# Modulation chunks 2 to 5 of a hybrid diffusion block: from scaled row sums and TensorE column sums to VectorE dots of transposed rows

## Chip, cores, metric

The kernel runs on one core of one Trainium2 chip. The metric is the device time of one execution in microseconds (us). All matrices are float32; each product is made of three float32r matmuls (high part by high part, high by low, low by high).

## What is computed

One layer of a diffusion transformer on 512 tokens of width 1024, with 256 context tokens. The part that matters here is the modulation: a conditioning row `c` of 1024 numbers goes through a SiLU and a 1024 by 6144 matrix, and the result is cut into six chunks of 1024 that shift, scale and gate the two halves of the layer.

```python
silu_c = jax.nn.silu(c)
mx = jnp.split((silu_c @ w_mod[l] + b_mod[l])[:, None, :], 6, axis=-1)
hx = modulate(rms_norm(x, g_mix[l]), mx[0], mx[1])
...
x = x + mx[2] * merge_branches(y_conv_x, att_x, gt_x, w_out[l])
hx2 = modulate(rms_norm(x, g_ffn[l]), mx[3], mx[4])
x = x + mx[5] * swiglu(hx2, w_13[l], w_2[l])
return rms_norm(x, g_final)
```

Chunks 0 and 1 are needed at the start, 2 at the output projection of the merge, 3 and 4 before the feed-forward part, 5 only at its second matrix.

## The kernel before

The layer is computed transposed: a tile holds 128 channels on the partitions and 512 tokens along the free axis. A weight tile is 128 by 1024 float32 (512 KB). `wtile` (L130) loads it on SP's DMA queue into one of three raw buffers `wr`, ScalarE casts it in two halves to float32r (`wh`, L118), and VectorE subtracts to get the low halves (`wl`, L122). There are six `wh` and six `wl` halves, so three tiles of weights. `gemm` (L138) then runs 8 times 3 matmuls of 128x512 (`mm3`, L134 to L136), 24 to a tile.

The order of the program around the change is:

1. eight attention heads, with the convolution's work between them; the last head leaves `o_t[7]` (L523);
2. the gate part: the remaining gates, each a tile of 24 matmuls and a Tanh (`gate`, L540 to L547); the sum of the eight convolution tiles (L857), its mean by a ones matmul (L860), then subtraction, squares and sums (L863 to L867), the variance's column sums (L187), `rstd_cols` (L170, and a power on GpSimd L172), and the broadcast of the result by another ones matmul (L177, L182);
3. the merge: the convolution tiles are scaled (L887) and pass a SiLU (L889), the heads are split in high and low parts (L101, L102); eight tiles with `w_o` (L896 to L901), eight with `w_pw` (L903 to L915), eight with `w_out` (L918 to L978);
4. the feed-forward part: 22 pairs of tiles with `w_13` (L1064 to L1076), then eight tiles of 22 products with `w_2`, and the final norm.

The code of 2, of 3 up to the fifth `w_out` tile, and of 4 up to the last `w_2` tile is not ordered by hand: the tile framework's scheduler puts each engine's instructions in an order of its own at compile time, by what it reckons to be ready, and gives out buffers in that order. Each engine then works its list in that order, and so does SP with its DMAs.

Modulation chunks 2 to 5 are `w_mod25[0]` to `[3]`. `mod_steps` (L202) makes a chunk in 16 steps: for each of 8 rows of input channels and each of two halves of 512 output channels, VectorE writes one column of a buffer of tag `p` (a copy from `after`, L207, which holds the step back until `after` exists), SP loads 256 KB (L208), and VectorE multiplies by a per-partition scalar of `sc` and adds to one of two accumulators (L210; L212 for the first). `mod_cols` (L220) then sums each accumulator over the partitions: 8 matmuls of 128x1 with a column of ones (L223; the profile shows two passes of each), and VectorE adds the bias (L225). The steps are handed out by `pump`: `MODS` says how many after each gate, each `w_o` tile and each `w_pw` tile (3, 3, 3), and `MCOLS` after which `w_pw` tile each chunk is finished. Chunk 5 is made by `mod_chunk` after the fifth pair of the feed-forward part (L1073) and finished after the fifteenth (L1075).

`row_dot` (L264) exists already: at the start chunk 1 is made by it. It multiplies a 128x1024 tile of transposed weights by a row that every partition holds, and sums along the row in the same instruction (`accum_out`). `md_tile` (L234) gives its buffers: tag `ur`, four of them, which are also used by the convolution's tap rows and by three of the residual tiles `x2` (L934).

Of the kernel before, what the change touches and what calls it, by code (L numbers as in the profile page):

```python
# [10 lines left out]
F32 = mybir.dt.float32  # L11
F32R = mybir.dt.float32r
AF = mybir.ActivationFunctionType
ALU = mybir.AluOpType
# [4 lines left out]
P = 128  # L19
D = 1024  # L20
KD = D // P
# [9 lines left out]
NB0 = 2  # L31
NB1 = 7
W_BUFS = 6
MODS = (3, 3, 3)
MCOLS = (2, 4, 7)
UPAD = 544
UW = 520
# [18 lines left out]
def block_kernel(ctx: ExitStack, tc: tile.TileContext, I, out):  # L56
    nc = tc.nc
    pe, act, dve, pool, sp = nc.tensor, nc.scalar, nc.vector, nc.gpsimd, nc.sync
# [24 lines left out]
    def slot(dt=F32, n=512):  # L83
        return ap.tile([P, n], dt, tag="act", name=nm("a"))
# [68 lines left out]
    def v(name, i=None, n=1):  # L153
        a, b = VEC[name]
        return vec[:, a:b] if i is None else vec[:, a + i:a + i + n]

    ones = cp.tile([P, P], F32, name="ones")
# [3 lines left out]
    sc = cp.tile([P, 16], F32, name="sc")  # L161
    act.activation(sc, vec[:, 0:16], AF.Silu)
    bm1 = cp.tile([P, 16], F32, name="bm1")
    dve.tensor_scalar(out=bm1[:, 0:8], in0=v("b_mod", 8, 8), scalar1=1.0, scalar2=None, op0=ALU.add)
    dve.tensor_scalar(out=bm1[:, 8:16], in0=v("b_mod", 32, 8), scalar1=1.0, scalar2=None, op0=ALU.add)
    modc = cp.tile([P, 32], F32, name="modc")
# [23 lines left out]
    def ps_x(n=512):  # L190
        return pp.tile([P, 512], F32, tag="x", name=nm("px"), bufs=4)[:, 0:n]
# [7 lines left out]
    def wide():  # L199
        return bp.tile([P, 768], F32, tag="p", name=nm("p"))  # L200

    def mod_steps(c, after, acc):  # L202
        acc += [slot(), slot()]
        for kc in range(8):
            for e in range(2):
                md = wide()[:, 0:512]
                dve.tensor_copy(out=md[:, 0:1], in_=after[:, 0:1])  # L207
                sp.dma_start(out=md, in_=I["w_mod25"][c, kc, :, e * 512:e * 512 + 512])  # L208
                if kc:
                    dve.scalar_tensor_tensor(out=acc[e], in0=md, scalar=sc[:, 2 * kc:2 * kc + 1], in1=acc[e], op0=ALU.mult, op1=ALU.add)  # L210
                else:
                    dve.tensor_scalar(out=acc[e], in0=md, scalar1=sc[:, 2 * kc:2 * kc + 1], scalar2=None, op0=ALU.mult)  # L212
                yield

    def mod_chunk(c, after):
        acc = []
        pump(mod_steps(c, after, acc), 99)
        return acc

    def mod_cols(c, acc):  # L220
        ps = ps_x(8)
        for i in range(8):
            pe.matmul(ps[:, i:i + 1], lhsT=acc[i // 4][:, (i % 4) * P:(i % 4 + 1) * P], rhs=ones[:, 0:1], start=True, stop=True)  # L223
        col = modc[:, c * 8:c * 8 + 8]
        dve.tensor_tensor(out=col, in0=ps, in1=bm1[:, 8:16] if c == 2 else v("b_mod", 16 + c * 8, 8), op=ALU.add)  # L225
        if c == 0:
            dve.tensor_scalar(out=col, in0=col, scalar1=0.5, scalar2=None, op0=ALU.mult)
        elif c == 2:
            dve.tensor_tensor(out=col, in0=col, in1=v("g_ffn", 0, 8), op=ALU.mult)
# [7 lines left out]
    def pads(tag):  # L237
        return bp.tile([P, 2, UPAD], F32R, tag=tag, name=nm(tag), bufs=1)

    def row_tile(j):  # L240
        t = pads(("u", "y")[j]).bitcast(F32).rearrange("p a b -> p (a b)")[:, 0:D]
        sp.dma_start(out=t, in_=I["crow"][:, j * D:j * D + D])
        return t

# [45 lines left out]
    def pump(it, n):  # L290
        for _ in range(n):
            if next(it, it) is it:
                break
# [4 lines left out]
    conv, o_t = [None] * KD, [None] * H  # L298
# [256 lines left out]
    with tc.manual_schedule(engines={ET.PE, ET.DVE, ET.Activation, ET.Pool, ET.SP}):  # L555
        for k in range(KD):
            t = slot()
# [24 lines left out]
        for k in range(KD):  # L582
# [17 lines left out]
            t = temp()  # L600
# [175 lines left out]
        for k in range(KD + 1):  # L776
            if k < KD:
                t = temp(C)
# [5 lines left out]
            if k:  # L784
                dve.scalar_tensor_tensor(out=hcs[k - 1][1], in0=ts[k - 1], scalar=ssc[:, k - 1:k], in1=hcs[k - 1][0].bitcast(F32),
                                         op0=ALU.add, op1=ALU.subtract)
# [63 lines left out]


    if True:
        maccs = [[], [], []]
        mods_it = itertools.chain(*(mod_steps(i, o_t[7], maccs[i]) for i in range(3)))
        tot = slot()
        for i in range(1, KD):
            dve.tensor_tensor(out=tot, in0=conv[0] if i == 1 else tot, in1=conv[i], op=ALU.add)  # L857
# [45 lines left out]
        for i in range(KD):  # L903
            w = wtile(I["w_pw"][i])
            ps = ps_x()
            gemm(ps, w, yc)
            t = sg_conv[i]
            dve.scalar_tensor_tensor(out=t, in0=t, scalar=1.0, in1=ps, op0=ALU.add, op1=ALU.mult)
            dve.tensor_tensor(out=t, in0=t, in1=m1[i], op=ALU.add)
            a, b = slot(F32R), slot(F32R)  # L910
            split(t, a, b)
            mg.append((a, b))
            pump(mods_it, MODS[2])
            if i in MCOLS:
                mod_cols(MCOLS.index(i), maccs[MCOLS.index(i)])  # L915


        HALF = (slice(0, 256), slice(256, 512))  # L918
# [147 lines left out]
        for j in range(2, KF):  # L1066
            ps = ps_s()
            pab = [ps[:, 0:512], ps[:, 512:1024]]
            for e, o in enumerate((j, KF + j)):
                w = wtile(I["w_13"][o])  # L1070
                gemm(pab[e], w, hx2)
            glu(*pab)
            if j == 4:  # L1073
                macc = mod_chunk(3, x2[0])
            if j == 14:  # L1075
                mod_cols(3, macc)  # L1076

        sq2 = slot()
        ssqs = [sq2[:, 0:256], sq2[:, 256:512]]
# [107 lines left out]
def _layout(i):  # L1187
# [20 lines left out]
        "w_mod0": mod[:, :, 0].transpose(2, 1, 0, 3).reshape(KD, P, D),  # L1208
        "w_mod1": i["w_mod"][0][:, D:2 * D].T.reshape(KD, P, D),
        "crow": np.broadcast_to(np.concatenate([i["c"].reshape(D), i["c_ctx"].reshape(D)]), (P, 2 * D)),  # L1210
        "w_mod25": mod[:, :, 2:6].transpose(2, 0, 1, 3, 4).reshape(4, KD, P, D),
        "w_kv": w_kv.reshape(KD, P, 384), "w_qa": _tiles(q),
        "w_in": _tiles(np.concatenate([kr, kr, kv, a, g, gc, gm], axis=1)),
        "w_uq": np.concatenate([qn[0], qr, uk[:, 0], qn[1], uk[:, 1]], axis=2),
# [46 lines left out]
```

## Time and profile before

| | us |
|---|---|
| median of 3 runs | 1018.43 |
| lowest and highest | 1016.11, 1018.98 |
| the profiled execution | 1017.07 |
| its span, first to last instruction | 1015.3 |
| TensorE busy in the span | 989.6 (97%) |
| VectorE busy | 601.8 (59%) |
| ScalarE busy | 430.0 (42%) |
| mean granted TensorE clock | 0.985 |

Busy times overlap, since the engines run beside each other. The granted clock is a share of full speed (2.4 GHz). A time in a list of instructions is counted from the start of the span.

### The profile page before, as it was taken

The page shows a single profiled execution, that of the slowest core. Times are in us where ns is not written, and L with a number is a line of the kernel's source. Part 1 is how long each engine was busy: PE and PEld are TensorE (multiplying, and loading weights), DVE is VectorE, ACT ScalarE, POOL GpSimd, SP SyncE. Part 2 cuts the span into 40 slices and gives each one's busy share as a digit, 9 for nine tenths or more (in the row PEclk, how much of TensorE's full clock was granted, in tenths as well). Part 3 has the DMA queues.
Part 4 walks back from the last instruction along what each step waited for, and adds up shares of the span by engine and source line. Part 5 has one row for each costly group of instructions (what it writes and reads, how often), then busy time and mean ns, then how long its engine had stood idle before and what let it go on. Part 6 is the DMA issues. An engine that isn't in the chain of part 4 may idle for free.

```text
span 1015.3 us, 13490 instructions
## 1 busy us (share of the span) xinstructions
PE 989.6 (97%) x5016; PEld 834.4 (82%) x5016; DVE 601.8 (59%) x1067; ACT 430.0 (42%) x798; POOL 102.6 (10%) x197
## 2 busy tenths in 40 slices
PE   8999899999999999999989999999999999999996
PEld 7878788888888887788778889888888888888886
DVE  5766579765986885426988854836534333333332
ACT  4352465555556556634642233533333233322222
POOL 0001210231423034100000001200000000000000
PEclk8998999999999999999999999999999999999998
DMA  9934542252623325432478551234433222333312
GB/s 328 397 106 141 167 143 77 70 145 70 162 80 94 100 58 132 145 104 83 156 249 276 188 178 63 103 105 144 167 103 103 84 103 85 94 99 94 94 57 83
DMA packets 49377, 132.82 MB, mean 131 GB/s; under 512 B 7520, under 2 KB 10720, under 8 KB 49312
## 3 DMA queue, kind: packets, MB, share of 16 engines
q1 hardware_dynamic: 42672, 115.27, 34.0%
q0 software_dynamic: 6640, 16.69, 7.0%
q8 instruction: 39, 0.64, 0.3%
q14 instruction: 26, 0.21, 0.1%
HBM read 113.16 MB, written 2.88 MB: 114 GB/s over the span
## 4 chain that ended last, share of the span: by engine, by line
PE 85%; issue 5%; DVE 5%; DMA 2%; ACT 1%; POOL 1%; SPq 0%; POOLq 0%; DVEq 0%; ACTq 0%
PE px L134 13%; PE px L135 12%; PE px L136 12%; PE ps L135 9%; PE ps L134 9%; PE ps L136 9%; PE px L305 8%; PE ps L492 3%; PE px L513 2%; PE ps L493 2%; PE px L271 1%; PE px L187 1%; PE ps L305 1%; DVE wl L122 1%; PE px L223 1%
## 5 line engine op out<-in xcount | busy, mean ns | idle before, releaser
L122 DVE TENSOR_TENSOR wl<-wr,wh 128x512 fp32r<-128x512 f32 (+1 forms) x284 | 189.6, 675 | 254.7 <-ACT wh L118 249.2
L118 ACT CAST wh<-wr 128x512 fp32r<-128x512 f32 (+1 forms) x290 | 174.3, 610 | 315.9 <-PE ps L135 132.7
L134 PE MATMUL px<-a,wh 128*128 128x512 f32 (+1 forms) x583 | 216.2, 373 | 3.8 <-ACT wh L118 2.9
L136 PE MATMUL px<-a,wl 128*128 128x512 f32 (+1 forms) x583 | 214.9, 370 | 2.9 <-DVE wl L122 2.9
L135 PE MATMUL px<-a,wh 128*128 128x512 f32 (+1 forms) x583 | 214.8, 369 | 0.0
L135 PE MATMUL ps<-a,wh 128*128 128x512 f32 (+1 forms) x376 | 141.6, 376 | 0.9 <-DVE a L1000 0.8
L134 PE MATMUL ps<-a,wh 128*128 128x512 f32 (+1 forms) x376 | 141.6, 376 | 0.0
L136 PE MATMUL ps<-a,wl 128*128 128x512 f32 (+1 forms) x376 | 141.2, 375 | 0.0
L134 PEld LDWEIGHTS px<-a,wh 128*128 128x128 f32 x583 | 110.9, 190 | 23.6 <-ACT wh L118 3.3
L136 PEld LDWEIGHTS px<-a,wl 128*128 128x128 f32 x583 | 111.1, 191 | 21.6 <-DVE wl L122 3.5
L135 PEld LDWEIGHTS px<-a,wh 128*128 128x128 f32 x583 | 110.9, 190 | 18.6 <-DVE a L102 0.4
L305 PE MATMUL px<-a,wh 128*128 128x512 f32 x320 | 101.8, 398 | 0.0
L135 PEld LDWEIGHTS ps<-a,wh 128*128 128x128 f32 x376 | 70.8, 188 | 14.3 <-DVE a L1000 1.5
L136 PEld LDWEIGHTS ps<-a,wl 128*128 128x128 f32 x376 | 70.8, 188 | 12.9
L134 PEld LDWEIGHTS ps<-a,wh 128*128 128x128 f32 x376 | 70.8, 188 | 12.6
L172 POOL TENSOR_TENSOR s<-s,mhalf 128x2 f32<-128x2 f32 (+1 forms) x10 | 9.6, 957 | 653.5 <-DVE s L170 653.5
L305 PEld LDWEIGHTS px<-a,wh 128*128 128x128 f32 x320 | 60.3, 191 | 12.8 <-issue 0.2
L344 DVE SCALAR_TENSOR_TENSOR a<-y,wd,a 128x512 f32<-128x512 f32 x90 | 67.1, 746 | 1.1
L305 PE MATMUL px<-a,wl 128*128 128x512 f32 x160 | 63.6, 398 | 0.0
L492 PE MATMUL ps<-a,a 128*128 128x512 f32 x160 | 58.3, 401 | 0.7 <-ACT e L367 0.4
L355 POOL DMA_DIRECT2D ur<-u x80 | 42.6, 538 | 106.3 <-DVE a L344 27.3
L369 POOL DMA_DIRECT2D a<-e x80 | 39.4, 498 | 91.3 <-ACT e L367 84.2
(213 smaller groups left out, 1384.0 us busy)
## 6 DMA issues: line engine op xcount, KB each, us to landing
wr<-in_w_dram SPq DMA_DIRECT2D x60, 512.0 KB, 3.5
wr<-in_w_in_dram SPq DMA_DIRECT2D x35, 512.0 KB, 3.6
p<-in_w_mod_dram SPq DMA_DIRECT2D x64, 256.0 KB, 3.8
ur<-u POOLq DMA_DIRECT2D x80, 130.0 KB, 3.5
md<-in_w_mod_dram SPq DMA_DIRECT2D x16, 512.0 KB, 6.2
a<-e POOLq DMA_DIRECT2D x80, 64.0 KB, 2.2
a<-in_w_mod_dram SPq DMA_DIRECT2D x16, 256.0 KB, 6.3
wr<-in_w_o_dram SPq DMA_DIRECT2D x8, 512.0 KB, 4.8
```

What stands on the lines that cost most here:

```text
L118: act.copy(h, raw[:, i * WB:i * WB + h.shape[-1]])
L122: (eng or dve).tensor_tensor(out=l, in0=raw[:, i * WB:i * WB + h.shape[-1]], in1=h.bitcast(F32), op=ALU.subtract)
L134: pe.matmul(ps, lhsT=wh, rhs=ah, start=first, stop=False)
L135: pe.matmul(ps, lhsT=wh, rhs=al, start=False, stop=False)
L136: pe.matmul(ps, lhsT=wl, rhs=ah, start=False, stop=last)
L305: pe.matmul(ps, lhsT=l, rhs=r, start=k == 0 and i == 0, stop=k == n - 1 and i == 2)
L344: dve.scalar_tensor_tensor(out=a, in0=u[:, t:t + S], scalar=w, in1=a, op0=ALU.mult, op1=ALU.add)
L355: pool.dma_start(out=ur[32 * s_:32 * s_ + 32].bitcast(F32), in_=u[32 * g:32 * g + 32, :, 8 * s_:8 * s_ + UW].bitcast(F32))
L369: pool.dma_start(out=parts[j][32 * g:32 * g + 32, :], in_=e[32 * j:32 * j + 32, j:j + S])
L492: pe.matmul(s[:, 0:512], lhsT=l[:, q0:q0 + P], rhs=rx_, start=i == 0, stop=i == 4)
L493: pe.matmul(s[:, 512:768], lhsT=l[:, q0:q0 + P], rhs=rc_, start=i == 0, stop=i == 4)
L513: pe.transpose(pt[:, qb * P:(qb + 1) * P], ps_[qb][:, kb * P:(kb + 1) * P], ident)
```

## The change

The weights of chunks 2 to 5 are laid out transposed, so that a 128x1024 tile holds 128 output channels with all 1024 input channels along the free axis. A chunk is then 8 steps instead of 16: one column copy, now by ScalarE; one load of 512 KB into a buffer of tag `ur`; one `row_dot` on VectorE, which leaves its sum in a column of `modc`. The row of `c` is loaded once more (512 KB) after the last head and passes a SiLU; its tile stays until the last dot. The accumulators and the matmuls with ones go away; `mod_cols` adds the bias only. Of the 24 steps of chunks 2 to 4 none is handed out after the gates, one after each `w_o` tile, two after each `w_pw` tile. Chunk 5 starts after the fourth pair of the feed-forward part, waits for the product tile `gt[2]` of the third, takes one step in each of eight pairs, and is finished after the twelfth.

```diff
-MODS = (3, 3, 3)
+MODS = (0, 1, 2)
...
-    def mod_steps(c, after, acc):
-        acc += [slot(), slot()]
-        for kc in range(8):
-            for e in range(2):
-                md = wide()[:, 0:512]
-                dve.tensor_copy(out=md[:, 0:1], in_=after[:, 0:1])
-                sp.dma_start(out=md, in_=I["w_mod25"][c, kc, :, e * 512:e * 512 + 512])
-                if kc:
-                    dve.scalar_tensor_tensor(out=acc[e], in0=md, scalar=sc[:, 2 * kc:2 * kc + 1], in1=acc[e], op0=ALU.mult, op1=ALU.add)
-                else:
-                    dve.tensor_scalar(out=acc[e], in0=md, scalar1=sc[:, 2 * kc:2 * kc + 1], scalar2=None, op0=ALU.mult)
-                yield
...
-    def mod_cols(c, acc):
-        ps = ps_x(8)
-        for i in range(8):
-            pe.matmul(ps[:, i:i + 1], lhsT=acc[i // 4][:, (i % 4) * P:(i % 4 + 1) * P], rhs=ones[:, 0:1], start=True, stop=True)
+    def mod_steps(c, after, row):
+        for k in range(KD):
+            md = md_tile()
+            act.copy(md[:, 0:1], after[:, 0:1])
+            sp.dma_start(out=md, in_=I["w_mod25"][c, k])
+            row_dot(md, row, modc[:, c * 8 + k:c * 8 + k + 1])
+            yield
+
+    def mod_cols(c):
         col = modc[:, c * 8:c * 8 + 8]
-        dve.tensor_tensor(out=col, in0=ps, in1=bm1[:, 8:16] if c == 2 else v("b_mod", 16 + c * 8, 8), op=ALU.add)
+        dve.tensor_tensor(out=col, in0=col, in1=bm1[:, 8:16] if c == 2 else v("b_mod", 16 + c * 8, 8), op=ALU.add)
...
-    def row_tile(j):
+    def row_tile(j, after=None):
         t = pads(("u", "y")[j]).bitcast(F32).rearrange("p a b -> p (a b)")[:, 0:D]
+        if after is not None:
+            act.copy(t[:, 0:1], after[:, 0:1])
         sp.dma_start(out=t, in_=I["crow"][:, j * D:j * D + D])
...
-        maccs = [[], [], []]
-        mods_it = itertools.chain(*(mod_steps(i, o_t[7], maccs[i]) for i in range(3)))
+        mrow = row_tile(0, o_t[7])
+        act.activation(mrow, mrow, AF.Silu)
+        mods_it = itertools.chain(*(mod_steps(i, o_t[7], mrow) for i in range(3)))
...
-            if j == 4:
-                macc = mod_chunk(3, x2[0])
-            if j == 14:
-                mod_cols(3, macc)
+            if j == 3:
+                mods_it = mod_steps(3, gt[2][0].bitcast(F32), mrow)
+            if 3 <= j < 11:
+                pump(mods_it, 1)
+            if j == 11:
+                mod_cols(3)
```

The scheduler's order moves with it. In the rows below the changed kernel's lines have other numbers: its `row_dot` is L253, the column copy L205; L877 is the former L887, L889 the former L899, L938 the former L948; L118, L122, L102 and L177 are unchanged. Of the tile names `md` and `p` are loaded modulation weights, `u` the row of `c`, `wr`, `wh` and `wl` weights (loaded, high, low), `px` and `ps` results in PSUM, `a` and `t` activations. In the changed kernel 14 of the 24 dots of chunks 2 to 4 stand ahead of the mean's subtraction on VectorE, 4 behind L177, and 6 in the `w_o` tiles.

VectorE from the broadcast of the norm (L177) to the first scaled convolution tile, before:

```order
L177 TENSOR_TENSOR t_4932<-cst,s_4930 128x512
L122 TENSOR_TENSOR wl_4997<-wr_4992,wh_4995 128x512
L207 COPY p_5028<-a_4433 128x1
L207 COPY p_5032<-a_4433 128x1
L122 TENSOR_TENSOR wl_5044<-wr_5040,wh_5042 128x512
L210 SCALAR_TENSOR_TENSOR a_4780<-p_4836,sc,a_4780 128x512
L122 TENSOR_TENSOR wl_5045<-wr_5040,wh_5043 128x512
L210 SCALAR_TENSOR_TENSOR a_4781<-p_4840,sc,a_4781 128x512
L207 COPY p_5036<-a_4433 128x1
L122 TENSOR_TENSOR wl_5092<-wr_5088,wh_5090 128x512
L207 COPY p_5076<-a_4433 128x1
L122 TENSOR_TENSOR wl_5093<-wr_5088,wh_5091 128x512
```

and with the change:

```order
L177 TENSOR_TENSOR t_4910<-cst,s_4908 128x512
L253 SCALAR_TENSOR_TENSOR md_5480,modc<-md_5480,u_4625 128x1024
L253 SCALAR_TENSOR_TENSOR md_5484,modc<-md_5484,u_4625 128x1024
L122 TENSOR_TENSOR wl_5054<-wr_5050,wh_5052 128x512
L253 SCALAR_TENSOR_TENSOR md_5529,modc<-md_5529,u_4625 128x1024
L253 SCALAR_TENSOR_TENSOR md_5533,modc<-md_5533,u_4625 128x1024
L877 TENSOR_TENSOR a_1429<-a_1429,px_4912 128x512
L102 TENSOR_TENSOR a_4875<-a_1783,a_4874 128x512
```

Five halves of `w_o` weights, two accumulations and four column copies stood between the broadcast and the scaling; now one half and four dots stand there.

VectorE during the first `w_o` tiles (`wl_5141` is the second half of the fourth tile), before:

```order
L210 SCALAR_TENSOR_TENSOR a_4780<-p_5080,sc,a_4780 128x512
L102 TENSOR_TENSOR a_4982<-t_4979,a_4981 128x512
L210 SCALAR_TENSOR_TENSOR a_4781<-p_5084,sc,a_4781 128x512
L102 TENSOR_TENSOR a_4989<-t_4986,a_4988 128x512
L210 SCALAR_TENSOR_TENSOR a_4780<-p_5124,sc,a_4780 128x512
L210 SCALAR_TENSOR_TENSOR a_4781<-p_5128,sc,a_4781 128x512
L207 COPY p_5132<-a_4433 128x1
L122 TENSOR_TENSOR wl_5141<-wr_5136,wh_5139 128x512
```

and with the change (`wl_5094`, `wl_5095` are the halves of the fourth tile, `wl_5134` and `wl_5135` those of the fifth; px_5060 is the result of the third):

```order
L102 TENSOR_TENSOR a_4932<-t_4929,a_4931 128x512
L122 TENSOR_TENSOR wl_5094<-wr_5090,wh_5092 128x512
L102 TENSOR_TENSOR a_4939<-t_4936,a_4938 128x512
L122 TENSOR_TENSOR wl_5095<-wr_5090,wh_5093 128x512
L102 TENSOR_TENSOR a_4946<-t_4943,a_4945 128x512
L122 TENSOR_TENSOR wl_5134<-wr_5130,wh_5132 128x512
L102 TENSOR_TENSOR a_4953<-t_4950,a_4952 128x512
L889 SCALAR_TENSOR_TENSOR a_4353<-a_4353,px_5060 128x512
```

The halves of the fourth tile now come right between the splits of the convolution tiles, and no modulation work stands ahead of them.

ScalarE in the feed-forward part, in one pair of tiles, before:

```order
L948 ACTIVATE t_6730<-ps_6661 128x512
L101 CAST a_6734<-t_6732 128x512
L118 CAST wh_6918<-wr_6916 128x512
L118 CAST wh_6919<-wr_6916 128x512
L118 CAST wh_6961<-wr_6959 128x512
L118 CAST wh_6962<-wr_6959 128x512
```

and with the change, where chunk 5 begins:

```order
L205 COPY md_6613<-a_6532 128x1
L118 CAST wh_6654<-wr_6652 128x512
L118 CAST wh_6655<-wr_6652 128x512
L205 COPY md_6694<-a_6532 128x1
L118 CAST wh_6701<-wr_6699 128x512
L118 CAST wh_6702<-wr_6699 128x512
L938 ACTIVATE t_6605<-ps_6536 128x512
L101 CAST a_6609<-t_6607 128x512
L118 CAST wh_6735<-wr_6733 128x512
L205 COPY md_6775<-a_6532 128x1
L118 CAST wh_6736<-wr_6733 128x512
L205 COPY md_6856<-a_6532 128x1
```

Eight column copies stand between the casts, two to a pair of tiles; each but the first waits for a dot on VectorE.

## Rows read from the trace of the kernel before

**Rows 1.** The page, part 1: busy time of each engine.
```profile
span 1015.3 us, 13490 instructions
...
PE 989.6 (97%) x5016; PEld 834.4 (82%) x5016; DVE 601.8 (59%) x1067; ACT 430.0 (42%) x798; POOL 102.6 (10%) x197
```

**Rows 2.** The chain that ended last: start, us, what ran.
```profile
473.15 0.86 PE px L860 x2
...
558.04 1.68 PE px L223 x16
...
804.56 1.68 PE px L223 x16
```

**Rows 3.** Timeline of TensorE, 555 to 562: start, us, instruction, [idle before].
```profile
557.65 0.39 PE L136 MATMUL px<-a,wl 128*128 128x512 f32 x1
557.88 1.84 PE L223 MATMUL px<-ones,a 128*128 128x1 f32 x16
559.58 0.49 PE L134 MATMUL px<-a,wh 128*128 128x512 f32 x1
559.90 0.40 PE L135 MATMUL px<-a,wh 128*128 128x512 f32 x1
```

**Rows 4.** Stretches: length, busy us (count) of PE, PEld, DVE, ACT, POOL, PEclk, DMA, GB/s.
```profile
430.00:470.00 40.00, 40.00 (x181) 32.44 (x180) 15.92 (x27) 14.16 (x27) 0.00 (x0) 1.00 0.29 96
...
518.00:520.00 2.00, 2.00 (x6) 1.60 (x5) 1.23 (x3) 0.00 (x0) 0.00 (x0) 0.50 0.85 238
```

**Rows 5.** Timeline of TensorE, 514 to 522.
```profile
516.70 0.50 PE L136 MATMUL px<-a,wl 128*128 128x512 f32 x1 [2.66 <-DVE wl L122]
...
520.91 0.40 PE L134 MATMUL px<-a,wh 128*128 128x512 f32 x1
```

**Rows 6.** Timeline of VectorE, 513 to 517.
```profile
513.31 0.74 DVE L210 SCALAR_TENSOR_TENSOR a<-p,sc,a 128x512 f32<-128x512 f32 x1
...
514.58 1.41 DVE L210 SCALAR_TENSOR_TENSOR a<-p,sc,a 128x512 f32<-128x512 f32 x2
...
515.97 0.68 DVE L122 TENSOR_TENSOR wl<-wr,wh 128x512 fp32r<-128x512 f32 x1
```

**Rows 7.** Groups of VectorE, 430 to 720: count, busy us, mean ns, idle before.
```profile
L210 DVE SCALAR_TENSOR_TENSOR a<-p,sc,a 128x512 f32<-128x512 f32 x56 | 41.1, 747 | 10.3 <-DMA p<-in_w_mod_dram 10.1
```

**Rows 8.** Timeline of VectorE, 97 to 101: dots of the program's start.
```profile
98.21 1.22 DVE L264 SCALAR_TENSOR_TENSOR md<-md,y 128x1024 f32<-128x1024 f32 x1
...
99.35 1.22 DVE L264 SCALAR_TENSOR_TENSOR md<-md,y 128x1024 f32<-128x1024 f32 x1
```

**Rows 9.** Timeline of VectorE, 468 to 494.
```profile
468.17 0.69 DVE L122 TENSOR_TENSOR wl<-wr,wh 128x512 fp32r<-128x512 f32 x1
...
487.43 0.69 DVE L177 TENSOR_TENSOR t<-cst,s 128x512 f32<-128x512 f32 x1 [0.94 <-POOL s L172]
...
492.62 0.68 DVE L887 TENSOR_TENSOR a<-a,px 128x512 f32<-128x512 f32 x1
493.21 0.68 DVE L102 TENSOR_TENSOR a<-a,a 128x512 fp32r<-128x512 f32 x1
```

**Rows 10.** Timeline of TensorE, 492 to 495.
```profile
493.06 0.97 PE L134 MATMUL px<-a,wh 128*128 128x512 f32 x3 [0.89 <-ACT a L101]
493.95 0.50 PE L135 MATMUL px<-a,wh 128*128 128x512 f32 x1
```

**Rows 11.** Who waited for whom: us in total, times, longest.
```profile
ACT wh L118 <- PE px L135: 128.5, 77, 2.6
```

**Rows 12.** Instructions on tile md at the start: their transfers' time to landing.
```profile
DMA to landing us min/median/max: 3.4/6.2/7.6
```

**Rows 13.** DMA issues, 699 to 722 and 740 to 800: count, KB, us to landing.
```profile
wr<-in_w_dram SPq DMA_DIRECT2D x4, 512.0 KB, 5.0
...
wr<-in_w_dram SPq DMA_DIRECT2D x11, 512.0 KB, 3.5
```

**Rows 14.** Groups of ScalarE, 0 to 60.
```profile
L570 ACT ACTIVATE u<-u 128x1024 f32<-128x1024 f32 x1 | 1.1, 1057 | 0.6 <-DMA u<-in_crow_dram 0.6
```

More of the change, by code (lines that the diff above doesn't have):

```diff
@@ L200, in wide @@
         return bp.tile([P, 768], F32, tag="p", name=nm("p"))
-    def mod_steps(c, after, acc):
-        acc += [slot(), slot()]
-        for kc in range(8):
-            for e in range(2):
-                md = wide()[:, 0:512]
-                dve.tensor_copy(out=md[:, 0:1], in_=after[:, 0:1])
-                sp.dma_start(out=md, in_=I["w_mod25"][c, kc, :, e * 512:e * 512 + 512])
-                if kc:
-                    dve.scalar_tensor_tensor(out=acc[e], in0=md, scalar=sc[:, 2 * kc:2 * kc + 1], in1=acc[e], op0=ALU.mult, op1=ALU.add)
-                else:
-                    dve.tensor_scalar(out=acc[e], in0=md, scalar1=sc[:, 2 * kc:2 * kc + 1], scalar2=None, op0=ALU.mult)
-                yield
[L215 to L218, printed above, removed]
-    def mod_cols(c, acc):
-        ps = ps_x(8)
-        for i in range(8):
-            pe.matmul(ps[:, i:i + 1], lhsT=acc[i // 4][:, (i % 4) * P:(i % 4 + 1) * P], rhs=ones[:, 0:1], start=True, stop=True)
+    def mod_steps(c, after, row):
[6 more added lines that the diff above has]
+    def mod_cols(c):
         col = modc[:, c * 8:c * 8 + 8]
-        dve.tensor_tensor(out=col, in0=ps, in1=bm1[:, 8:16] if c == 2 else v("b_mod", 16 + c * 8, 8), op=ALU.add)
+        dve.tensor_tensor(out=col, in0=col, in1=bm1[:, 8:16] if c == 2 else v("b_mod", 16 + c * 8, 8), op=ALU.add)
         if c == 0:
@@ L914, in block_kernel @@
             if i in MCOLS:
-                mod_cols(MCOLS.index(i), maccs[MCOLS.index(i)])
+                mod_cols(MCOLS.index(i))
         HALF = (slice(0, 256), slice(256, 512))
@@ L1210, in _layout @@
         "crow": np.broadcast_to(np.concatenate([i["c"].reshape(D), i["c_ctx"].reshape(D)]), (P, 2 * D)),
-        "w_mod25": mod[:, :, 2:6].transpose(2, 0, 1, 3, 4).reshape(4, KD, P, D),
+        "w_mod25": i["w_mod"][0][:, 2 * D:].T.reshape(4, KD, P, D),
         "w_kv": w_kv.reshape(KD, P, 384), "w_qa": _tiles(q),
```

## The prediction

> **What bounds the kernel now.** I read the page's part 1 first: TensorE is busy 989.6 of 1015.3 us, so only what stands on TensorE, or makes it wait, can move the end [rows 1]. Next the chain that ended last: it follows TensorE through the merge and the feed-forward part, and it holds the modulation's own matmuls as four stretches of 1.68 us, three in the merge (558 the first) and one at 804 [rows 2]. Then TensorE's timeline about one of these stretches [rows 3] and about its longest wait in the merge [rows 5], with VectorE's timeline beside it [rows 6]. From 430 to 470 TensorE never pauses, while VectorE works 15.9 and ScalarE 14.2 of 40 us, and the DMA engines 29% [rows 4]: what lies there has cover.
>
> A matmul of 128x512 starts 0.23 us after the one before (557.65 to 557.88) [rows 3], so a tile of 24 takes 5.5 us. There are three tiles of weights, and the casts mostly wait for TensorE to give a half back (77 waits of this kind on px tiles, none over 2.6 us) [rows 11]. A half that is cast when its buffer comes free is used two and a half tiles later, some 13.6 us. That is the cover of everything which the change puts on ScalarE, VectorE and SP beside plain tiles.
>
> **The change part by part.** The profiled execution took 1017.07 us, its span 1015.3; it lies 1.36 us under the median of 1018.43. The sum is made against 1017.07.
>
> *The column sums go.* From the first of the 16 to the next ordinary matmul it is 559.58 - 557.88 = 1.70 us, and the gap after that one is 0.32 instead of 0.23: 1.8 us that TensorE does not pay without them [rows 3]. Nothing else runs on TensorE then, and their operands were ready. Four groups: **-7.2 us**. The row's 16 instructions in 1.70 us are 106 ns each. The Trainium skill, "TensorE: Matmul & The Clock Gate", section "Back-to-back issue gap", gives about 81 ns for pairs of weight load and matmul at 128 columns and less time for fewer; by that a group would be an estimated 1.3 us and this term -5.2. The trace differs, and the measured 106 ns decides.
>
> *The stall at 514 goes.* In the fourth `w_o` tile TensorE waits 2.66 us for a `wl` half on VectorE [rows 5]. VectorE was not idle: it worked through accumulations of modulation (513.31, and two at 514.58) and began that half only at 515.97 [rows 6]. After the wait the granted clock is 0.50 from 518 to 520 [rows 4], the lower level of 1.2 GHz, and 11 matmuls take from 516.70 to 520.91, 4.21 us instead of 11 x 0.23 = 2.5: 1.7 us lost. With the change no modulation work stands between the convolution splits at that place; by the order the fourth tile's halves come ahead of the fifth split, the fifth tile's close behind. The 56 accumulations of 0.75 us [rows 7] become dots of 1.14 us start to start (98.21 to 99.35) [rows 8], one for every two: VectorE has less to do in the merge, not more. What is late next there is nothing: stepping VectorE's list on from 493.2 with 0.6 us an entry (492.62 to 493.21) [rows 9], the halves of the fourth tile are done at about 508, and TensorE, which does tiles one to three first, asks for them at about 510. Bounds: all of it back, -4.4; or the wait only moves to another half, 0. I take **-4.4**, because the instructions that made it wait are gone from that place.
>
> *Four dots ahead of the scaling.* Behind L177 (its successor can start at 488.04) VectorE now does four dots and one half: 4 x 1.14 + 0.6 = 5.2, so L887 starts at 493.2 instead of 492.62, and the first head's low part comes 0.6 later [rows 9]. TensorE starts its first three matmuls at 493.06 after 0.89 us of waiting as now, and the fourth, which wants that low part, started at 493.95, right when VectorE had it [rows 10]. So the delay is paid: **+0.6 us**. Bounds: 0, and 0.6 + 1.7 if the two short waits together bring the clock down; a wait of 0.89 alone did not, 2.66 did [rows 5, 10].
>
> *The gate part.* Though no step is handed out there, the order puts 14 dots ahead of the mean. Cost on VectorE: 14 x 1.14 = 16 us of the 24 that are free between 430 and 470 [rows 4]. What counts is the sum of the convolution tiles, which must be done by 473.15 [rows 2]. The last half but one ahead of it is paced by TensorE (468.17 now [rows 9]); behind it two additions and a dot, 0.6 + 0.6 + 1.1, make 471.2. The dots' own loop: four buffers, so dot 13 comes three rounds after dot 1. Dot 1 needs the row and its SiLU (1.06 us [rows 14]), at about 437 + 3.5 + 1.1 = 441.6. A round is a landing, a dot and up to one cast step of 2.7 us on ScalarE, where the copy for the next load stands behind casts. With a landing of 3.5 [rows 13], 3 x 7.4 = 22 us: dot 13 at 464. With 6.2, the median at the crowded start [rows 12], 3 x 10.1 = 30: at 472, a bit late (about 0.8 us at the mean). SP's queue gets 18 loads more of 512 KB, its other loads wait behind them in order, and ScalarE's casts behind copies that wait for dots; all inside 13.6 us of cover. I take **0**; bounds 0 and +6.8 (landing 7.6, the start's longest: three times 1.4 more, and 1.7 of clock).
>
> *The feed-forward part.* Three of the four `ur` buffers hold residual tiles there, so chunk 5 has one, and each column copy on ScalarE waits for the dot before it. A loop is landing + 1.14 + a few tenths: 3.5 gives about 5, under the 5.5 us of a tile. Eight dots add 9 us to VectorE in 43. **0**; bounds are priced below.
>
> *The rest.* The table load of the SiLU moves from the merge to the gate part, its number unchanged by the order. The merge's 48 and the feed-forward's 16 column copies leave VectorE; 32 and the row's go to ScalarE, which has room [rows 1]. Residual tiles five to seven wait for the last dots of chunk 4 to give back their buffers; those dots stand ahead of the last three `w_o` results on VectorE, and `w_out` comes eight `w_pw` tiles later.
>
> Sum: -7.2 - 4.4 + 0.6 = -11.0, from 1017.07 to 1006.1; from the median it would be 1007.4. The one profiled execution is a draw among the three, so I put the forecast between, at **1007.0 us**.
>
> **Rivals.**
>
> *The stall comes back elsewhere.* For it: the scheduler has rearranged the whole merge, and VectorE has no gap in the rows ahead of the half that was late [rows 6]. Against: the modulation work there shrinks. Price: the same 2.66 + 1.7 at another half, so -7.2 + 0.6: 1010.5 to 1011.8. If only the clock falls after two short waits, 1008. The Trainium skill, "TensorE: Matmul & The Clock Gate", section "What's actually happening", says that the cost of warming up varies from run to run and is not to be fitted; the trace has one such fall to show, and what it says would add or take 1.7 us here.
>
> *The gate part is not free.* The change does not keep the dots out of it. Landing times near those of the start make the mean late by 0.8 to 5.1 us, with the clock 1.7 more: 1007 to 1013. For it: 18 loads of 512 KB and the row in 37 us beside 96 GB/s that are there already. Against: rows 12 are from a start with a longer queue.
>
> *Slower: one buffer in the feed-forward part.* ScalarE's copies wait for dots; its casts and SiLUs, and VectorE's `wl`, stand behind them. If a loop is longer than 5.5 us, ScalarE falls behind in seven loops by 7 x (loop - 5.5). TensorE has two pairs of result tiles, so it feels what exceeds two tiles, 11 us. Landing 3.5: no loss. Landing 5.0, as in the burst of chunk 5 now [rows 13]: loop 6.4, behind by 7, no loss. Landing 6.2: loop 7.6, 15 - 11 = 4, with the clock 1.7: 1012. Landing 7.6: loop 9, 24.5 - 11 = 13.5, with 1.7: 1021. From a landing of about 7.5 us on the kernel would be slower than before. Against: the weights there land in 3.5 us [rows 13], and the change doubles that traffic, no more.
>
> **How the numbers follow.** Forecast as summed: 0.62. The stall elsewhere: 0.20. The gate part: 0.08. The feed-forward loop: 0.10, of which half ends slower. The range goes from 1004.0 (the lowest of the three runs, 1016.11, less the 11.6 of the two gains, rounded) to 1012.0 (the median with the first gain alone, and the better half of the other two rivals). A measurement of this kernel can tell about 0.3% from no change, 3 us here. Forecast, stall elsewhere, gate part and a little of the feed-forward rival lie below 1015.4: faster 0.86; the rest of it is within 3 us (0.09) or above (0.05).
>
> **What would show it.** Right: no L223 left and TensorE's busy time down by about 7 us; no TensorE wait over 1 us between 490 and 530 and a granted clock of 1.00 there; L887 starting about 0.6 us later against the mean; TensorE without a pause in the feed-forward pairs. Wrong: a TensorE wait for `wl` or `wh` in the `w_o` tiles; the mean's matmul waiting for VectorE; waits of ScalarE for dots that add up over the eight pairs until TensorE pauses.

## The result, and the profile after

The changed kernel took 1011.08 us, the median of 20 executions (1007.14 to 1018.04), against 1017.99 for the kernel before beside it: ratio 0.9946, 95% interval 0.9928 to 0.9963. The medians lie 6.9 us apart, the means 5.7. The kernel is faster, by 0.5% where 1.1% was forecast; 1011.08 lies within the range given, 4 us above the value.

The granted clock of the first 130 us differs between executions of one and the same kernel (from 20 to 50 us it was 0.51 in e2 and 0.90 in e10 below, which are one kernel), and moves the whole time by up to 10 us; so traces are compared here over one stretch behind that, from the last wait of attention to the end. The row is TensorE's last wait for a cast of the probabilities. Its start, taken from the span, gives 1014.0 - 437.33 = 576.67 us for e2 and 1003.4 - 426.69 = 576.71 for e10. The row of e2:

```profile
core 0 of [0], span 1014.0 us
...
437.33 0.50 PE L134 MATMUL px<-ph,a 128*128 128x512 f32 x1 [1.02 <-ACT ph L101]
```

In the kernel before that row starts at 427.63 of 1015.3, which leaves 587.67 us; in the changed kernel at 427.01 of 1007.8, which leaves 580.79: 6.9 us less, where the terms of the forecast made 11.0. All the runs are told by this stretch. The row, and TensorE's last wait but one, at the matmul L187 of the last norm, in the kernel before:

```profile
427.63 0.50 PE L134 MATMUL px<-ph,a 128*128 128x512 f32 x1 [1.01 <-ACT ph L101]
...
1005.94 0.61 PE L187 MATMUL px<-ones,t 128*128 128x1 f32 x4 [1.09 <-ACT t L1142]
```

and in the changed kernel:

```profile
427.01 0.50 PE L134 MATMUL px<-ph,a 128*128 128x512 f32 x1 [1.02 <-ACT ph L101]
...
998.52 0.61 PE L187 MATMUL px<-ones,t 128*128 128x1 f32 x4 [1.08 <-ACT t L1134]
```

One piece of the stretch is still uneven: what stands behind that second row, the last 10 us, took 9.3 to 10.5 us in the twelve traces. It was 9.4 in e9 and 10.5 in e2, though their code there is the same. So the experiments also give the stretch without it.

The page of the changed kernel, part 1 (beside [rows 1]): TensorE has 64 instructions and 7.9 us less, VectorE 8.8 us less.

```profile
span 1007.8 us, 13259 instructions
...
PE 981.7 (97%) x4952; PEld 826.7 (82%) x4952; DVE 593.0 (59%) x1003; ACT 435.8 (43%) x832; POOL 102.9 (10%) x197
```

Stretches of the changed kernel: length, busy us (count) of PE, PEld, DVE, ACT and POOL, then PEclk, DMA share and GB/s. Its times run 0.6 us ahead of those of the kernel before from the last wait of attention on (427.01 against 427.63).

```profile
436.00:472.00 36.00, 36.00 (x161) 29.81 (x160) 24.09 (x43) 15.44 (x42) 0.00 (x0) 1.00 0.84 304
472.00:476.00 4.00, 1.34 (x6) 0.67 (x4) 4.00 (x8) 1.50 (x4) 0.00 (x0) 0.97 0.63 206
476.00:478.00 2.00, 2.00 (x5) 1.24 (x4) 2.00 (x5) 0.19 (x1) 0.00 (x0) 0.50 0.91 350
478.00:480.00 2.00, 2.00 (x7) 1.57 (x7) 2.00 (x4) 1.83 (x3) 0.00 (x0) 0.71 0.76 234
...
505.00:530.00 25.00, 25.00 (x112) 20.66 (x111) 24.65 (x44) 14.04 (x29) 0.00 (x0) 1.00 0.56 186
650.00:800.00 150.00, 150.00 (x672) 124.56 (x671) 66.44 (x103) 51.69 (x93) 0.00 (x0) 1.00 0.39 129
```

The place of the old stall, now inside 505 to 530, is full at a clock of 1.00, and so is the feed-forward part. But TensorE has a new hole at 472 to 476 and a fall of the clock behind it: (1 - 0.50) x 2 + (1 - 0.71) x 2 = 1.6 us. The gate part ahead of it moves 304 GB/s at a DMA share of 0.84 (96 and 0.29 before [rows 4]). TensorE's timeline names the wait: the matmul of the mean waits for the last addition of the convolution tiles (L847). The two short waits at the start of `w_o` follow it, and the second is the one that was forecast.

```profile
475.18 1.51 PE L850 MATMUL px<-a,ones 128*128 128x512 f32 x2 [2.66 <-DVE a L847]
...
496.96 0.95 PE L134 MATMUL px<-a,wh 128*128 128x512 f32 x3 [0.89 <-ACT a L101]
498.46 0.50 PE L135 MATMUL px<-a,wh 128*128 128x512 f32 x1 [0.55 <-DVE a L102]
```

The chain that ended last (start, us, what) goes through two transfers there: 6.32 and 7.37 us long, each followed by the dot that it feeds, and the additions stand behind. Between the two stand dot 8, a half of a gate's weights on VectorE, a copy on ScalarE that waits for it, and a weight load on SP's queue; the load of dot 11 leaves right behind that.

```profile
449.28 6.32 DMA md<-in_w_mod_dram
...
457.45 1.23 DVE md L253 x2
458.67 0.62 DVE wl L122
...
459.31 0.20 ACT wr L526
...
459.53 0.33 SPq L527
...
459.90 7.37 DMA md<-in_w_mod_dram
...
474.43 0.62 DVE a L847
475.04 0.14 issue
475.18 1.51 PE px L850 x2
```

VectorE's timeline: dots 1, 5, 9 and 13, the wait for dot 11, and the last addition, which stands behind dot 13. Between the seven additions there are three dots.

```profile
443.32 1.23 DVE L253 SCALAR_TENSOR_TENSOR md<-md,u 128x1024 f32<-128x1024 f32 x1 [5.00 <-ACT u L843]
...
450.32 1.22 DVE L253 SCALAR_TENSOR_TENSOR md<-md,u 128x1024 f32<-128x1024 f32 x1
...
461.20 1.23 DVE L253 SCALAR_TENSOR_TENSOR md<-md,u 128x1024 f32<-128x1024 f32 x1 [1.64 <-DMA md<-in_w_mod_dram]
...
467.29 1.23 DVE L253 SCALAR_TENSOR_TENSOR md<-md,u 128x1024 f32<-128x1024 f32 x1 [1.30 <-DMA md<-in_w_mod_dram]
...
473.20 1.22 DVE L253 SCALAR_TENSOR_TENSOR md<-md,u 128x1024 f32<-128x1024 f32 x1
...
474.35 0.69 DVE L847 TENSOR_TENSOR a<-a,a 128x512 f32<-128x512 f32 x1
```

DMA issues from 430 to 480: the 18 loads of the modulation landed in a median of 6.3 us and the row in 4.6. The Trainium skill, "DMA: Bandwidth & Descriptors", section "Anatomy of one DMA — SWDGE (gpsimd) path", fits a single transfer, one that GpSimd issues, as 2.0 us and its bytes at 436 GB/s; for these 512 KB, which SP issues, that would be an estimated 3.2 us. The quiet 3.5 of [rows 13] comes near it; the loads of the gate part, beside each other, took nearly twice as long.

```profile
md<-in_w_mod_dram SPq DMA_DIRECT2D x18, 512.0 KB, 6.3
...
u<-in_crow_dram SPq DMA_DIRECT2D x1, 512.0 KB, 4.6
```

### The profile page after: what moved, and what is told of

Read it like the earlier page. It is cut to its first block, busy times and chain, and to the rows that moved or that the text cites. A ratio compares the mean times of both kernels' runs of the same rounds, so it can differ in the third digit from the quotient of the medians.

```text
span 1007.8 us, 13259 instructions
## 1 busy us (share of the span) xinstructions
PE 981.7 (97%) x4952; PEld 826.7 (82%) x4952; DVE 593.0 (59%) x1003; ACT 435.8 (43%) x832; POOL 102.9 (10%) x197
## 4 chain that ended last, share of the span: by engine, by line
PE 88%; DVE 6%; DMA 3%; issue 2%; ACT 1%; SPq 0%; POOLq 0%; POOL 0%; DVEq 0%; ACTq 0%
PE px L134 13%; PE px L135 12%; PE px L136 12%; PE px L294 9%; PE ps L135 9%; PE ps L136 9%; PE ps L134 9%; PE ps L481 4%; PE px L502 2%; PE ps L482 2%; PE px L260 2%; DMA md<-in_w_mod_dram 1%; DVE md L253 1%; PE px L187 1%; DVE wl L122 1%
## 5 line engine op out<-in xcount | busy, mean ns | idle before, releaser
L122 DVE TENSOR_TENSOR wl<-wr,wh 128x512 fp32r<-128x512 f32 (+1 forms) x284 | 190.3, 676 | 239.4 <-ACT wh L118 234.3
L118 ACT CAST wh<-wr 128x512 fp32r<-128x512 f32 (+1 forms) x290 | 174.4, 610 | 281.8 <-PE ps L135 129.8
L253 DVE SCALAR_TENSOR_TENSOR md<-md,u 128x1024 f32<-128x1024 f32 x40 | 48.5, 1221 | 13.7 <-DMA md<-in_w_mod_dram 8.6
```

Source lines behind the costliest of these rows:

```text
L118: act.copy(h, raw[:, i * WB:i * WB + h.shape[-1]])
L122: (eng or dve).tensor_tensor(out=l, in0=raw[:, i * WB:i * WB + h.shape[-1]], in1=h.bitcast(F32), op=ALU.subtract)
L253: dve.scalar_tensor_tensor(out=md, in0=md, scalar=1.0, in1=row, op0=ALU.mult, op1=ALU.mult, accum_out=col)
```

## The experiments

The theory behind them: the dots between the additions wait for transfers, the mean comes 2.7 us late and the clock falls behind the wait; the rest of the forecast holds. The rivals were execution-to-execution differences (A), casts that ScalarE holds back (B, G, H), a bill that only moves with the dots (C), and a loss in the feed-forward part (D).

Every trace in three pieces, in us: from the last wait of attention to the first matmul of `w_o` (the row with the wait of 0.89), from there to the matmul L187 of the last norm, and the last 10 us.

| | to `w_o` | to the last norm | the end |
|---|---|---|---|
| before | 65.43 | 512.88 | 9.36 |
| changed | 69.95 | 501.56 | 9.28 |
| e7, changed again | 67.72 | 501.53 | 9.77 |
| e1 | 66.20 | 501.61 | 9.29 |
| e2 | 65.42 | 500.79 | 10.46 |
| e10, as e2 | 65.42 | 500.91 | 10.38 |
| e3 | 65.44 | 501.24 | 10.27 |
| e9 | 65.42 | 501.23 | 9.36 |
| e6 | 70.19 | 501.52 | 9.84 |
| e4 | 65.42 | 508.18 | 9.35 |
| e8 | 70.06 | 503.34 | 9.88 |
| e5 | 65.44 | 527.87 | 9.87 |

The first piece is the same to 0.02 in the kernel before and in the six runs without a new wait there. So what the changed kernel adds to it, 4.5 us and in e7 2.3, belongs to the gate part. The second piece is 11.3 us shorter in the changed kernel both times; the terms of the forecast, all of which lie there, make 11.0.

All executions can be set beside this by an estimate: the span of each times its mean granted clock is about its time at full clock. The mean of it is 999.6 us for the kernel before (66 executions beside the runs), 992.2 and 992.6 for the changed kernel (20, and 9 in e7), 991.5 for e1, and 989.2 to 989.9 for e2, e3, e9 and e10, with standard errors of 0.3 or less. So the changed kernel is some 3 us behind those four over many executions too, of which about 0.5 is the short wait at `w_o`; what the lower clock costs comes on top.

**e1: the additions ahead of the dots.** The sum gets a buffer that is free earlier, and the order then has all seven additions ahead of the first dot.

```diff
-        tot = slot()
+        tot = wide()[:, 0:512]
```

> The seven additions of the sum for the mean stand ahead of the dots on VectorE (the sum has another buffer); everything else is the changed kernel. Theory (the dots delay the sum, TensorE waits 2.66 us for it at 475 and its clock then falls, about 1.7 us): the wait on the mean is under 0.3 us, no granted clock under 0.8 between 470 and 485 us, and the time is 4 to 5 us under the changed kernel's: about 1006.5 us against 1018.0 for the kernel before, ratio 0.989. Rival A (the rest of the forecast is lost to something that differs from execution to execution, not to this wait): the wait goes, but the median stays at 1010 to 1012, ratio 0.993 to 0.995. Rival B (weight casts behind the copies on ScalarE, not the additions, are what is late): TensorE waits as long as before at 470 to 480 us for a cast or another operand, and the time is within 1 us of the changed kernel's.

Measured: 1010.03 us, ratio 0.9919 (0.9889 to 0.9949). Stretch 577.10 us, 3.7 less than the first trace of the changed kernel, all of it in the first piece. No wait on the mean and no fall of the clock, though dots and transfers stay in the gate part. TensorE's three waits of the merge, one of them new, for the sum of squares, which dots now delay:

```profile
484.88 1.05 PE L187 MATMUL px<-ones,a 128*128 128x1 f32 x8 [0.53 <-DVE a L857]
...
493.30 0.99 PE L134 MATMUL px<-a,wh 128*128 128x512 f32 x3 [0.89 <-ACT a L101]
494.87 0.50 PE L135 MATMUL px<-a,wh 128*128 128x512 f32 x1 [0.58 <-DVE a L102]
```

The theory's wait stands, and rival B falls. The median came out above the 1006.5 expected and inside the 1010 to 1012 that rival A named, though the ratio is not in A's 0.993 to 0.995. Medians of 12 executions move with the clock of the start; the price of 3.7 us rests on one trace of each kernel, and by the estimate over all executions e1 is about 1 us under the changed kernel, without the clock.

**e2 and e10: all 24 dots behind the sum of squares.** The same kernel twice.

```diff
-        mods_it = itertools.chain(*(mod_steps(i, o_t[7], mrow) for i in range(3)))
...
+        mods_it = itertools.chain(*(mod_steps(i, ssq, mrow) for i in range(3)))
```

> The 24 dots of the merge wait for the sum of squares (about 482 us), so none of their transfers, copies or products lies in the gate part. Theory: the additions are done by 471 us, no wait on the mean, no fall of the clock at 476; the two to six dots that the order now has ahead of the scaling cost at most 1.5 us at 492 to 499; time 1006 to 1008 us against 1018.0, ratio 0.988 to 0.990. Rival A (execution to execution): 1010 to 1012. Rival C (the dots' bill moves with them: 24 dots and their transfers beside the scaling and the casts stall TensorE there by 3 us or more): no better than the changed kernel, with waits at 490 to 560 us.

> The kernel of the run in which all 24 dots wait for the sum of squares, once more and with more executions, beside the same executions of the kernel before. Theory: stretch from the last wait of attention to the end 576.2 to 577.2 us again (no wait on the mean in any execution), median 1006 to 1009, ratio 0.988 to 0.991. Rival A (one lucky execution): a stretch over 578 us.

Measured: 1008.09 us, ratio 0.9903 (0.9868 to 0.9937), and 1009.65, 0.9917 (0.9887 to 0.9948). Stretches 576.67 and 576.71 us: 11.0 less than the kernel before and 4.1 less than the changed kernel. That the forecast's sum was 11.0 too is chance: these runs do not pay its 0.6 at `w_o`, and their last 10 us came out a microsecond longer. Ahead of those they are 12.1 and 12.0 us shorter than the kernel before. Both medians are a little above what was expected (1008 and 1009), and so are the ratios; the clock of the start moves them. The gate part and the place of the mean in e10:

```profile
436.00:472.00 36.00, 36.00 (x160) 29.84 (x159) 13.43 (x20) 13.96 (x25) 0.00 (x0) 1.00 0.32 103
472.00:476.00 4.00, 4.00 (x17) 2.96 (x16) 3.35 (x6) 3.14 (x6) 0.00 (x0) 1.00 0.39 116
```

TensorE never pauses there, at 103 GB/s. The only wait of the merge that is left is the 0.89 of the kernel before [rows 10].

**e3: all 24 dots behind the first result of `w_o`.** `o_t[7]` becomes `sg_mla[0]` in the same line.

> The 24 dots wait for the first result of the output projection of attention (about 503 us): none lies in the gate part or ahead of the scaling. Theory: no wait on the mean, and TensorE's waits at 496 to 499 us (0.89 and 0.55) are those of the kernel before (0.9 to 1.1 in all); time 1005 to 1007 us against 1018.0, ratio 0.987 to 0.989. Rival A: 1010 to 1012. Rival C (the dots' bill moves with them): waits of 3 us or more at 505 to 575 us, where ScalarE has seven copies in a row that wait for dots, and no gain.

Measured: 1006.95 us (6 executions), ratio 0.9871 (0.9837 to 0.9905). Stretch 576.95 us. Waits of 0.89 and 0.29 at the start of `w_o`, none at 505 to 575, where VectorE and the DMA engines now are at their busiest. Rival C falls with e2 and e3: the same dots cost nothing elsewhere.

**e9: only chunk 2 in the gate part.** The first eight dots as in the changed kernel, the other 16 behind the sum of squares.

```diff
-        mods_it = itertools.chain(*(mod_steps(i, o_t[7], mrow) for i in range(3)))
+        early = mod_steps(0, o_t[7], mrow)
...
+        mods_it = itertools.chain(early, *(mod_steps(i, ssq, mrow) for i in (1, 2)))
```

> The changed kernel with only the first chunk's eight dots in the gate part; the other 16 wait for the sum of squares. The order has all eight dots ahead of the first addition and none between the additions. Theory (the cost is the dots that stand between the additions and wait for transfers there, not dots and transfers in the gate part as such): in the changed kernel the eighth dot ends 31.6 us behind the last wait of attention and seven additions take 4.5 us more, so the sum stands at about 37 us where TensorE wants it at 45.5: no wait on the mean, and the stretch from the last wait of attention to the end is 576.5 to 577.5 us. Rival H (any dots ahead of the additions cost, by ScalarE's held casts): a wait of over 0.5 us at the mean or at a gate's weights, stretch over 578 us.

Measured: 1007.67 us, ratio 0.9911 (0.9881 to 0.9940). Stretch 576.01 us, half a microsecond under the range expected and the shortest of all, but only by its last 10 us; ahead of those e2 and e10 are 0.3 to 0.4 shorter. No wait on the mean. The last additions on VectorE (the last wait of attention stands at 435.99 here):

```profile
471.69 2.14 DVE L847 TENSOR_TENSOR a<-a,a 128x512 f32<-128x512 f32 x3
...
474.41 2.14 DVE L847 TENSOR_TENSOR a<-a,a 128x512 f32<-128x512 f32 x3
```

They end at 476.55, 40.5 us behind it, later than the 37 expected and still 5 us ahead of TensorE. So eight dots and their transfers ahead of the additions are free; with the ones between them gone, so is the wait. Rival H falls.

**e6: the column copies on GpSimd.** They leave ScalarE, where the weight casts stand behind them.

```diff
-            act.copy(md[:, 0:1], after[:, 0:1])
+            (pool.tensor_copy(out=md[:, 0:1], in_=after[:, 0:1]) if c < 3 else act.copy(md[:, 0:1], after[:, 0:1]))
```

> The changed kernel with the column copies of the merge's dots on GpSimd, which is idle there, in place of ScalarE; the order on VectorE stays but for three rows. Theory F (the dots wait for transfers of 6.3 us through four buffers, and the additions stand behind the dots): TensorE still waits 2 us or more for the mean, and the stretch from the last wait of attention to the end stays at 580 to 581 us (580.79 in the changed kernel). Theory G (the copies hold the weight casts on ScalarE, and VectorE's additions stand behind a residue that waits for a held cast): the wait on the mean falls under 1 us, no fall of the clock, and the stretch is 577 to 578 us.

Measured: 1012.22 us, ratio 0.9924 (0.9896 to 0.9952). Stretch 581.55 us, no better than the changed kernel and half a microsecond over the range of theory F.

```profile
477.27 1.11 PE L850 MATMUL px<-a,ones 128*128 128x512 f32 x2 [2.92 <-DVE a L847]
```

The wait on the mean is as long as it was, and the clock falls behind it. The copies on ScalarE are not the cause (G falls). The order on SP's queue is the same as in the chain shown above: the load of dot 11 leaves at 463.34, behind a weight load at 462.90.

**e7: the changed kernel again.**

> The changed kernel once more, beside the kernel before on the same chip. Theory (the wait on the mean stands in every execution, the rest of the spread is the clock of the first 130 us): wait of 2 to 3 us at the mean and half clock behind it, stretch from the last wait of attention to the end 580.3 to 581.3 us, median 1009 to 1012. Rival A (it differs from execution to execution): a wait on the mean under 1.5 us, or a stretch under 579 us.

Measured: 1012.88 us, ratio 0.9955 (0.9922 to 0.9988). Stretch 579.02 us, not the theory's 580.3 to 581.3, and the median is above its 1012. The wait is under the 1.5 us that rival A named, so on the size of the wait A was right: it differs between executions.

```profile
478.95 1.10 PE L850 MATMUL px<-a,ones 128*128 128x512 f32 x2 [1.38 <-DVE a L847]
```

The stretch behind it:

```profile
479.00:481.00 2.00, 2.00 (x7) 1.34 (x8) 2.00 (x4) 0.69 (x3) 0.00 (x0) 1.00 0.99 369
```

The wait stands, but it is 1.38 us and the clock stays at 1.00. In this execution VectorE does not wait for the transfer of dot 11, which cost 1.30 in the first one. Without it 1.38 us of the wait are left; the rest, with the fall of the clock, by these two traces hangs on when a single transfer lands. The theory was too rigid; the gate part costs 2.3 us here and 4.5 in the first trace (the first piece of the table).

**e4: chunk 5 alone by dots,** in the kernel before.

```diff
+        mrow = row_tile(0, o_t[7])
+        act.activation(mrow, mrow, AF.Silu)
...
-            if j == 4:
-                macc = mod_chunk(3, x2[0])
-            if j == 14:
-                mod_cols(3, macc)
+            if j == 3:
+                mods_it = dot_steps(3, gt[2][0].bitcast(F32), mrow)
+            if 3 <= j < 11:
+                pump(mods_it, 1)
+            if j == 11:
+                dot_cols(3)
```

> The kernel before, with chunk 5 alone by dots behind the third feed-forward tile (chunks 2 to 4 as before). Theory (a group of column sums costs TensorE 1.8 us where it stands, the loop of dots in the feed-forward part nothing): 1.7 us under the kernel before, ratio 0.998, and no wait of TensorE over 0.2 us at 650 to 800 us. Rival D (the feed-forward part takes away some of the forecast gain): at or above the kernel before, ratio 1.000 or more. Rival A: within 0.3% either way and nothing to be read from it.

Measured: 1015.54 us, ratio 0.9963 (0.9933 to 0.9992). Stretch 582.95 us: 4.7 less than the kernel before where 1.7 was expected. The run isn't pure: the row's load and SiLU shift the planned order, and the stall at 514 shrinks though its chunk is done the old way.

```profile
511.39 0.50 PE L134 MATMUL px<-a,wh 128*128 128x512 f32 x1 [0.93 <-ACT wh L118]
```

That is 2.66 - 0.93 = 1.7 of waiting, and 1.7 more because the clock stays at 1.00; with one group, 1.8, that makes 5.2, where 4.7 was measured. The run bears out the size of the old stall by accident, and TensorE has no wait from 650 to 800 us (D falls).

**e8: the changed kernel with chunk 5 in the old way.** Its products and column sums stand again where e4 took them out.

> The changed kernel with chunk 5 in the old way (products, then a group of column sums in the feed-forward part). Theory (the loop of dots in the feed-forward part costs nothing and spares one group): the stretch from the last wait of attention to the end is 1.8 us longer than in the changed kernel, 582.6 us, and TensorE has no wait over 0.2 us at 650 to 800 us in either. Rival D (the loop of dots costs TensorE something there): no longer than the changed kernel's 580.8 us.

Measured: 1010.83 us, ratio 0.9918 (0.9887 to 0.9950). Stretch 583.28 us, 2.5 more than the changed kernel. The second piece is 1.8 longer, the group; the rest is the last 10 us (0.6) and a slightly longer wait on the mean (2.72). Its median lies under the changed kernel's, inside the spread that the start's clock makes. TensorE has no wait from 650 to 800 in either. The loop of dots there costs nothing.

**e5: each column sum twice,** in the kernel before.

```diff
             pe.matmul(ps[:, i:i + 1], lhsT=acc[i // 4][:, (i % 4) * P:(i % 4 + 1) * P], rhs=ones[:, 0:1], start=True, stop=True)
+            pe.matmul(ps[:, i:i + 1], lhsT=acc[i // 4][:, (i % 4) * P:(i % 4 + 1) * P], rhs=ones[:, 0:1], start=True, stop=True)
```

> The kernel before with each column-sum matmul of the four groups issued twice (64 instead of 32). Measured is the stretch from the last wait of attention (427.63 us in the kernel before, 587.67 us to the end), since the clock of the first 130 us differs from execution to execution. Theory (a group costs TensorE 1.8 us where it stands): four more groups, 7.2 us more: 594.9 us, and L223 x32 a group. Rival E (part of a group is hidden: an added matmul of one column costs less than the 106 ns that the first ones show): under 592 us.

Measured: 1039.07 us, ratio 1.0158 (1.0103 to 1.0212). Stretch 603.18 us, 15.5 more than the kernel before, not 7.2. A doubled group takes 571.07 - 567.52 = 3.55 us to the next ordinary matmul, twice the 1.7 to 1.8 of [rows 3], so the price of the instructions is as expected. What comes on top is the clock: behind each of the four it falls.

```profile
567.52 0.28 PE L223 MATMUL px<-ones,a 128*128 128x1 f32 x2
...
571.07 0.78 PE L134 MATMUL px<-a,wh 128*128 128x512 f32 x1
```

The stretches beside and behind this first group:

```profile
566.00:570.00 4.00, 4.00 (x31) 3.73 (x30) 3.21 (x8) 1.50 (x3) 0.00 (x0) 1.00 0.69 205
570.00:574.00 4.00, 4.00 (x18) 3.42 (x18) 3.69 (x7) 0.62 (x1) 0.00 (x0) 0.62 0.34 114
```

At 0.62 over 4 us it loses 1.5 us there; the stretches behind the other three lose 1.7, 1.7 and 2.9. Together 7.8, and 7.2 makes 15.0, as much as the second piece has grown.

## Why the prediction was right and where it was wrong

**The column sums: right.** No L223 is left, TensorE is busy 7.9 us less, and e8 (1.8 in the second piece) and e5 (3.55 for a double one) give the price of one. At single length a group brings no fall of the clock, at double length it does.

**The stall at 514: right.** TensorE is full from 505 to 530 at a clock of 1.00. The two terms make 11.6. In the second piece of the table e2 and e10, which have no second wait at `w_o`, are 12.1 and 12.0 under the kernel before; e3 and e9, which pay 0.29, 11.6 to 11.7; the changed kernel, which pays 0.55, 11.3.

**Four dots ahead of the scaling: right, +0.6 forecast and 0.55 measured.** The clock did not fall behind the two short waits.

**The feed-forward part: right, nothing.** The loads of chunk 5 landed in 4.0 us. ScalarE waited for dots as the prediction said, up to 3.0 us, inside the cover of the result tiles. Who waited for whom from 655 to 800, us in total, times and longest:

```profile
ACT md L205 <- DVE md L253: 11.4, 4, 3.0
```

**The gate part: wrong, the step that failed.** It was taken at 0 and cost 4.5 us in the first trace and 2.3 in e7. The mechanism was in the text, and so was a size near the truth: with landings of 6.2 us it put dot 13 at 472. But I chose 3.5, from a quiet stretch of the feed-forward part [rows 13], for a stretch into which the change itself puts 18 loads and a row. They landed in 6.3 (5.9 in e7). Counted from the last wait of attention, dot 1 came at 16.3 us instead of 14.0: the row landed in 4.6, and the table load of the SiLU, 1.28 us, which had been put down as unchanged, now stood ahead of the first dot. Dot 13 came at 46.2, where the slow case of the text has 44.4, 1.8 sooner. TensorE wants the mean at 45.5 in both kernels. So the "0.8 us at the mean" of the text and 1.8 for the dot make the 2.6 that were measured. And the fall of the clock, 1.6 us, was kept for the upper bound alone.

That the slow case came so near is in part luck. Dot 13 did not wait for its own transfer, its row has no wait. Dot 11 did, and behind it VectorE worked without a pause through three dots, two halves of weights and five additions, from 467.29 to 474.95. Nor was the third part of a round the cast step on ScalarE: e6 takes the copies away from there and gains nothing, and by the chain the load of dot 11 left SP's queue 3.0 us after dot 7 had ended because it stood behind a weight load, which waited for VectorE, which was at dot 8. No run gave the dots' loads more buffers or another queue, so how the cost divides between landing time and this order is not shown.

**The rivals.** "The gate part is not free" was the right one and had a chance of 0.08; its 1007 to 1013 holds the median. That the range of the prediction holds it too is luck: its upper end, 1012.0, came mainly from the first gain without the second, and both gains came. "The stall comes back elsewhere" named a time that holds the median (1010.5 to 1011.8), but at the wrong place, a weight half in `w_o`; no such wait came. The slower rival needed landings of 7.5 us in the feed-forward part; they were 4.0.

**What beats both kernels.** Keeping the dots off the additions: e9 (0.9911), e2 and e10 (0.9903 and 0.9917) and e3 (0.9871). By the stretch they are 11 to 12 us under the kernel before and 4 to 5 under the first trace of the changed kernel. Their intervals overlap, and e3's six executions all had a high clock (0.982 to 0.986 over the span, where the others go down to 0.975), so none is shown the best of them.

## What to carry to other kernels

Price a moved transfer with the landing time of a stretch as crowded as the one that it will make, not of a quiet one, and look at what stands ahead of it in its queue. Work that is cheap on an idle engine still costs when the engine is in order and the piece waits for a transfer: look for the short critical instructions that the planner puts between such pieces (here seven additions of 0.6 us), and put those first or hold the pieces back. A count of free microseconds (16 of 24) says nothing about where in the row the wait falls.

## What the runs showed of the hardware

Behind a wait of 2.66 us (also 2.72 and 2.92) the granted clock went to 0.50, the level of 1.2 GHz; behind 1.38 and 0.93 it stayed at 1.00. The length of a wait does not decide alone: the waits of 1.08 and 1.58 us in the last norm are the same in all twelve traces, and behind them the last two matmuls took 0.67 us in six traces and 1.11 to 1.19 in the other six. The changed kernel has the first:

```profile
1000.71 0.67 PE L1119 MATMUL px<-t,ones 128*128 128x256 f32 x2 [1.58 <-DVE t L1111]
```

and e10 the second:

```profile
995.20 1.19 PE L1118 MATMUL px<-t,ones 128*128 128x256 f32 x2 [1.58 <-DVE t L1110]
```

The granted clock of the 4 us from L187 on was 0.86 and 0.77 there.

The case that was not expected is e5: TensorE had no pause at all, its row shows it fully busy, and still 32 matmuls of one column in 3.55 us brought the clock to its lower level in all four places (0.50 from 571 to 574 at the first), where 16 in 1.7 us did not. The Trainium skill, "TensorE: Matmul & The Clock Gate", section "HAM oscillation — how this bites in real kernels", gives gaps in which TensorE is idle as what makes it fall. The waits at the mean agree with that as far as the falls stand behind gaps; e5 has a fall without a gap, so a busy row in the profile is no sign that the clock will hold.
